# A two-layer encoder trunk: gains packed with the first x tiles on a second DMA queue, rotary tables on VectorE, the residual fetched during the second projection, and the last output block written by column chunks

## The chip, the cores and the metric

The kernel runs on one core of a Trainium2 chip. A core has a matmul engine (TensorE; PE in the profile, with its weight loads as PEld), VectorE (DVE), ScalarE (ACT), GpSimd (POOL), a queue that issues transfers (SyncE; SP), and 16 DMA engines that move data between HBM and the on-chip memory (SBUF). Matmuls write to PSUM, from where DVE or ACT read. The engines run side by side and wait for each other on semaphores. The metric is the time of one execution in microseconds (us); lower is better.

## The reference

The input is 256 tokens of width 2048 in float32. Two layers are computed; each adds a mixer and then a gated MLP to the residual x. In the first layer:

```python
h = rms_norm(x, norm_mix[layer])
proj = h @ w_in_ab[e]           # pooling channels | 12 query heads | 4 key heads | 4 value heads
q = apply_rope(rms_norm(q, q_norm[e]), cos, sin)
k = apply_rope(rms_norm(k, k_norm[e]), cos, sin)
pool_out = multiscale_pool(u, pool_w[e], pool_scale[e])
att_out = blocked_gqa(q, k, v)
x = x + concat(pool_out, att_out) @ w_out_ab[e]
x = x + conv_ffn(rms_norm(x, norm_ffn[layer]), w_up, conv_w, conv_b, w_down)
```

The second layer has an mLSTM mixer in the place of the attention and the same kind of MLP. All weights are read once, 410 MB in all.

## The kernel before

**Numbers.** The matmuls take a reduced float32 type (fp32r). To keep precision, each operand is written as a high part and a low part, and each product is three matmuls: high x high, high x low, low x high. So every weight that comes from HBM is first split: ACT casts it to the high part (L87), DVE subtracts that from the weight to get the low part (L88).

**Weights.** `Stream` reads the weights as chunks of 128 x 1024 floats (512 KB) in the order of use. `load` (L78) issues a chunk's transfer on SP's queue into one of 6 buffers `w`, `split` makes the two parts in one of 4 buffers `hl`, and `next` gives a chunk to the matmuls, after it has loaded up to 5 chunks and split 1 or 2 ahead. A moving chunk serves two slices of 128 input features: 12 matmuls of 512 columns, in kproj, qproj, vproj and the down projections.

**The start.** ACT's queue fetches the norm gains, `gcol` (32 KB, L176). SP's queue fetches the transposed x in eight transfers of 256 KB, two feature slices each (L178), with the first weight chunks between them; the first chunk comes in halves. Five matmuls on a zeroed tile (L215) run meanwhile. `Norm.parts` makes the high part (ACT, L251) and the low part (DVE, L252) of a slice of x times its gain. The scale of the norm, one factor per token, is applied after the projections. kproj (the keys) is the first projection, then qproj of the first four heads, vproj, and the other eight query heads.

**During kproj and after it.** When kproj's chunks have been issued, the program reads the residual, x with tokens on the partitions, in four transfers of 512 KB (L578), sums the squares of each block on ACT (`squares`, L259), and reads the first constants (L581) and the rotary tables `katt` (L583). POOL multiplies the tables by the q and k gains (L588). The `k_block` then squares the key heads on ACT (`hsq_k`, L391), rotates them on DVE (L400 to L403, `rot_k`), gets the norm's scale from the sums of squares (DVE, with one power on POOL, L198), scales (`rot_k`, L425), transposes on PE (`tr_k`, L434) and splits into `kt`. A `q_block` does the same for four query heads, and then `head` does scores, softmax, a transposition of the probabilities (`ptr`, L475) and the product with v.

**What sets the order.** The order on PE is written out by hand. `Weave` keeps small tasks (blocks, heads) as generators with a due time in estimated us; each time that a group of matmuls is written, `tick` advances the clock and may put one due step between. A `yield 5.5` is such an estimate. On the other engines a planner sets the order, except where the program pins it: ACT and DVE are pinned up to the end of kproj. A queue is served in order, so what stands behind a waiting instruction waits too. SP has at most eight transfers on their way, since each semaphore is waited for before it is used again.

**The end.** The down projection of the second MLP writes four blocks of 512 columns. The last, `down_end`, does all matmuls of the first 128 tokens, adds to x (DVE, L880) and writes out (L881), and then those of the other 128 tokens, with two additions and two writes of 256 columns. Both token halves lie in one PSUM tile, and in the program the matmuls of the second half wait for the addition of the first.

Of the kernel before, what the change touches and what calls it, by code (L numbers as in the profile page):

```python
# [9 lines left out]
F32 = mybir.dt.float32  # L10
# [6 lines left out]
P = 128  # L17
D = 2048
S = 256
KT = D // P  # L20
# [44 lines left out]
class Stream:  # L65
# [15 lines left out]

    def split(self):
        i = self.n_split
        w, n = self.w.pop(i)
        hl = self.spool.tile([P, 2, CH * P], F32R, tag="hl", name=f"hl{i}")
        for c in range(0, CH * P, n):
            self.nc.scalar.copy(hl[:, 0, c : c + n], w[:, c : c + n])  # L87
            self.nc.vector.tensor_sub(hl[:, 1, c : c + n], w[:, c : c + n], hl[:, 0, c : c + n].bitcast(F32))  # L88
        self.hl[i] = hl
        self.n_split += 1  # L90
# [62 lines left out]
@with_exitstack  # L153
def trunk(ctx: ExitStack, tc: tile.TileContext, xT, xn, gains, call, catt, cml, wgate, weights, out):
    nc = tc.nc
# [24 lines left out]
    ctx.enter_context(tc.manual_schedule(engines={mybir.EngineType.PE}))  # L180

    wv = Weave()
# [3 lines left out]
    def gain(n, k):  # L186
        c = n * KT + k
        return gcol[:, c : c + 1]
# [19 lines left out]

    warm = actp.tile([P, 512], F32, tag="B0", name="warm")
    v.memset(warm, 0.0)  # L210
# [3 lines left out]
    for i in range(WARM):  # L214
        pe.matmul(wps[:, :256], warm[:, :P], warm[:, :256], start=True, stop=True, skip_group_check=True)  # L215

    class Norm:
# [31 lines left out]
        def parts(self, j, src):  # L249
            n = self.n  # L250
            a.activation(self.xx[:, j, 0, :], src, AF.Copy, scale=gain(n, j))  # L251
            v.scalar_tensor_tensor(  # L252
                self.xx[:, j, 1, :], src, gain(n, j),
                self.xx[:, j, 0, :].bitcast(F32), ALU.mult, ALU.subtract)
# [62 lines left out]
    def mov_group(act, name, width=512, before=None, after=None):  # L317

        ps = mmp.tile([P, 2, width], F32, tag="mm", name=name)
        per = CH * P // width  # L320
        hl = None
        for k in range(KT):
            if k % per == 0:
                before and before(k)
                hl = st.next()
                after and after(k)
            src = act(k)
            c = (k % per) * width
            for t in range(2):
                xh, xl = src[:, 0, t * P : t * P + P], src[:, 1, t * P : t * P + P]  # L330
                o = ps[:, t, :]
                first, last = k == 0 and (width == 512 or t == 0), k == KT - 1 and (width == 512 or t == 1)
                mm(o, xh, hl[:, 0, c : c + width], first, False)
                mm(o, xh, hl[:, 1, c : c + width], False, False)
                mm(o, xl, hl[:, 0, c : c + width], False, last)
            wv.tick(1.29 * width / 512)
        return ps
# [33 lines left out]
    def attention_layer(norm, nxt):  # L371
        with ExitStack() as es:
# [11 lines left out]
            def block(ps, ti, dst, name):  # L384
# [32 lines left out]
                rq = None  # L417
                if name == "k":
                    fin = norm.finish()
                    yield next(fin)  # L420
                    rq = scales()
                    yield 4.0
                    for t in range(2):
                        r4 = rot[:, t, :].rearrange("p (h d) -> p h d", h=4)
                        v.tensor_mul(r4, r4, rq[:, 4 * t : 4 * t + 4].unsqueeze(2).to_broadcast([P, 4, P]))  # L425
                    yield 3.0
# [18 lines left out]
            def head(h, qt, hh, kt, vt, rq):  # L445
# [51 lines left out]
            def ahead(k):  # L497
                if k + 3 < KT:
                    norm.parts(k + 2, a_x[:, k + 2])
                    norm.parts(k + 3, a_x[:, k + 3])  # L500

            done = set()
# [77 lines left out]
            norm.blocks = NB  # L580
            nc.sync.dma_start(cst[:, :C_CONV], call[:, :C_CONV])  # L581
            kc = tp.tile([P, A_PW], F32, tag="rot", name="katt")
            nc.sync.dma_start(kc, catt[:, :A_PW])  # L583

            for i in range(4):
                gn = kc[:, A_QN + i * P : A_QN + (i + 1) * P]
                tr = kc[:, A_COS + (i % 2) * 2 * P : A_COS + (i % 2 + 1) * 2 * P]
# [10 lines left out]
            v.tensor_sub(vt[:, 1], vf, vt[:, 0].bitcast(F32))  # L598
            nc.sync.dma_start(cst[:, C_CONV:], call[:, C_CONV:])

# [231 lines left out]
    def ffn_layer(layer, norm, nxt):  # L832
        with ExitStack() as es:
# [31 lines left out]
            def down_end(gt, b, kts):  # L865

                ps = mmp.tile([P, 2, 512], F32, tag="mm", name="end")
                hls = [st.next() for _ in range(len(kts) // 2)]
                for t in range(2):
                    for k in kts:  # L870
                        c = k % 2 * 512
                        wh, wl = (hls[k // 2][:, j, c : c + 512] for j in range(2))
                        xh, xl = (gt[:, k, j, t * P : t * P + P] for j in range(2))
                        mm(ps[:, t], xh, wh, k == kts[0], False)
                        mm(ps[:, t], xh, wl, False, False)
                        mm(ps[:, t], xl, wh, False, k == kts[-1])
                    for c in range(0, 512, 512 // (1 + t)):
                        n = 512 // (1 + t)
                        xs = x[:, t, b * 512 + c : b * 512 + c + n]
                        v.tensor_add(xs, xs, ps[:, t, c : c + n])  # L880
                        nc.sync.dma_start(out[:, t, b * 512 + c : b * 512 + c + n], xs)  # L881

# [201 lines left out]
```

## Time and profile before

| what | value |
|---|---|
| time, median of 3 runs | 2217.97 us (2217.95 to 2218.12) |
| the profiled execution's time | 2218.25 us |
| its span in the profile | 2216.0 us |
| PE busy | 2205.2 us (100%) |
| PEld busy | 1887.1 us (85%) |
| DVE, ACT, POOL busy | 1527.6, 1169.5, 33.4 us |
| DMA | 415.45 MB, mean 187 GB/s |

The span goes from the first to the last event that the profiler saw on the core; the time also has what lies around it. A matmul's end is modelled, so a busy PE is not a PE at its peak. In a row of the timeline stand the start, the length, the engine, the line of the program, the operation with its output and inputs, the count, and in brackets how long the engine idled before it and who released it. The chain of work that ended last goes back from the last instruction to what released each step. The list of waits sums who waited for whom, as a total, a count and the longest.

### The profile page before, as it was taken

The numbers are of one execution on the slowest core, as the hardware profiler recorded it, in microseconds if no ns is written. First come the engines' busy times: TensorE is split into PE (matmuls) and PEld (weight loads), VectorE is DVE, ScalarE is ACT, GpSimd is POOL, SyncE is SP. The second block draws the span as 40 slices with busy tenths as digits, with TensorE's granted clock in tenths as the row PEclk, the third lists the DMA queues.
The fourth block names the chain that finished last, engine by engine and source line by source line (L and its number), as shares of the span: only waits on it lengthen the run. The fifth ranks groups of instructions, "written<-read, shape, count | busy, mean of one in ns | idle before, by whom it ended". The sixth has DMA issues, their size and how long they took to land.

```text
span 2216.0 us, 30515 instructions
## 1 busy us (share of the span) xinstructions
PE 2205.2 (100%) x11650; PEld 1887.1 (85%) x11650; DVE 1527.6 (69%) x2174; ACT 1169.5 (53%) x1662; POOL 33.4 (2%) x39
## 2 busy tenths in 40 slices
PE   8999999999999999999999999999999999999999
PEld 7888888888888888888888889888888888888887
DVE  7676677776676767666777676667777677676764
ACT  6665555554554545455554554455555455454542
POOL 1011000000000000000000000000000000000000
PEclk9999999999999999999999999999999999999999
DMA  8555566666666666654566555556656666666664
GB/s 317 167 165 163 177 190 189 191 190 192 190 191 190 191 191 189 196 188 156 178 193 186 180 183 171 184 178 190 190 190 190 190 190 191 190 190 190 190 191 141
DMA packets 117877, 415.45 MB, mean 187 GB/s; under 512 B 13115, under 2 KB 15587, under 8 KB 117731
## 3 DMA queue, kind: packets, MB, share of 16 engines
q1 hardware_dynamic: 114656, 410.02, 58.5%
q10 hardware_dynamic: 3074, 3.48, 0.7%
q8 instruction: 91, 1.49, 0.3%
q14 instruction: 56, 0.45, 0.1%
HBM read 411.31 MB, written 2.14 MB: 187 GB/s over the span
## 4 chain that ended last, share of the span: by engine, by line
PE 98%; ACT 1%; DVE 1%; DMA 0%; issue 0%; SPq 0%; DVEq 0%; ACTq 0%
PE up L191 44%; PE dn L191 21%; PE op L191 8%; PE mk L191 4%; PE mq L191 4%; PE mo L191 4%; PE mv L191 4%; PE qproj L191 3%; PE vproj L191 1%; PE kproj L191 1%; PE qk L191 1%; PE av L191 1%; PE end L191 1%; PE pool L191 0%; PE xt L242 0%; PE ov L191 0%
## 5 line engine op out<-in xcount | busy, mean ns | idle before, releaser
L88 DVE TENSOR_TENSOR hl<-w,hl 128x1024 fp32r<-128x1024 f32 (+1 forms) x769 | 937.7, 1220 | 470.7 <-ACT hl L87 469.1
L87 ACT CAST hl<-w 128x1024 fp32r<-128x1024 f32 (+1 forms) x769 | 806.7, 1050 | 683.7 <-PE dn L191 241.2
L191 PE MATMUL up<-xx,hl 128*128 128x512 f32 (+1 forms) x5632 | 984.2, 337 | 0.0
L191 PEld LDWEIGHTS up<-xx,hl 128*128 128x128 f32 x5632 | 857.9, 188 | 125.8
L191 PE MATMUL dn<-hl,g 128*128 128x512 f32 x2064 | 471.3, 389 | 0.0
L191 PEld LDWEIGHTS dn<-hl,g 128*128 128x128 f32 x2064 | 386.2, 188 | 79.5
L342 ACT COPY tb_up<-up 128x512 f32<-128x512 f32 x88 | 51.7, 587 | 154.0 <-PE up L191 154.0
L343 DVE TENSOR_TENSOR tb_up<-up,tb_up 128x512 f32<-128x512 f32 x88 | 60.9, 692 | 97.0 <-ACT tb_up L342 97.0
L854 ACT ACTIVATE y<-tb_up,cst 128x256 f32<-128x256 f32 x176 | 96.4, 595 | 46.9 <-DVE tb_up L850 46.9
L191 PE MATMUL mk<-xx,hl 128*128 128x512 f32 (+1 forms) x512 | 92.4, 338 | 0.0
L191 PE MATMUL mq<-xx,hl 128*128 128x512 f32 (+1 forms) x512 | 92.0, 337 | 0.0
L191 PE MATMUL op<-hl,cat 128*128 128x512 f32 x384 | 91.7, 393 | 0.0
L191 PE MATMUL mo<-hl,xx 128*128 128x512 f32 (+1 forms) x480 | 91.6, 348 | 0.0
L191 PE MATMUL mv<-hl,xx 128*128 128x512 f32 x384 | 89.6, 391 | 0.0
L191 PE MATMUL op<-hl,mcat 128*128 128x512 f32 x384 | 89.5, 392 | 0.0
L191 PEld LDWEIGHTS mq<-xx,hl 128*128 128x128 f32 x512 | 79.3, 188 | 11.7
L191 PEld LDWEIGHTS mk<-xx,hl 128*128 128x128 f32 x512 | 79.1, 188 | 11.4
L191 PEld LDWEIGHTS mo<-hl,xx 128*128 128x128 f32 x480 | 76.5, 190 | 10.6
L191 PEld LDWEIGHTS mv<-hl,xx 128*128 128x128 f32 x384 | 71.7, 188 | 14.8
L191 PEld LDWEIGHTS op<-hl,mcat 128*128 128x128 f32 x384 | 71.4, 188 | 14.6
L191 PEld LDWEIGHTS op<-hl,cat 128*128 128x128 f32 x384 | 70.9, 188 | 14.1
L857 DVE SCALAR_TENSOR_TENSOR y<-tb_up,cst,y 128x255 f32<-128x255 f32 x176 | 76.9, 479 | 0.0
(207 smaller groups left out, 1293.3 us busy)
## 6 DMA issues: line engine op xcount, KB each, us to landing
w<-in_up SPq DMA_DIRECT2D x352, 512.0 KB, 3.6
w<-in_dn SPq DMA_DIRECT2D x176, 512.0 KB, 4.0
w<-in_m_in SPq DMA_DIRECT2D x128, 512.0 KB, 3.6
w<-in_a_in SPq DMA_DIRECT2D x47, 512.0 KB, 4.1
w<-in_a_out SPq DMA_DIRECT2D x32, 512.0 KB, 3.4
w<-in_m_out SPq DMA_DIRECT2D x32, 512.0 KB, 3.4
xT<-in_xT SPq DMA_DIRECT2D x8, 256.0 KB, 6.9
x<-in_xn SPq DMA_DIRECT2D x4, 512.0 KB, 8.6
```

The costliest lines, as they stand in the source:

```text
L87: self.nc.scalar.copy(hl[:, 0, c : c + n], w[:, c : c + n])
L88: self.nc.vector.tensor_sub(hl[:, 1, c : c + n], w[:, c : c + n], hl[:, 0, c : c + n].bitcast(F32))
L191: pe.matmul(out_, lhsT, rhs, start=start, stop=stop, skip_group_check=True)
L342: a.copy(tb, ps[:, :, 1, :])
L343: v.tensor_add(tb, ps[:, :, 0, :], tb)
L854: a.activation(y[:, j, :], u[:, j, :], AF.Identity, scale=cw(tl, 1), bias=cw(tl, 3))
L857: v.scalar_tensor_tensor(y[:, j, 0 : S - 1], u[:, j, 1:S], cw(tl, 2), y[:, j, 0 : S - 1], ALU.mult, ALU.add)
```

## The change

- The gains and the first two slices of x are packed in one array `gx`, read with one transfer on ACT's queue into `gx0`; the next two slices of x follow on that queue. POOL copies the gains to `gcol`; the first two slices take their gains from `gx0`.
- SP's queue starts with the first two weight chunks, both in halves. The rest of x and the weights follow in turn.
- The very first cast, of half a chunk, is on DVE. The first six matmuls of kproj go by kind (both token halves high x high, then high x low, then low x high). The low part of the first slices is made between the two halves of the first chunk (`then`).
- The zeroed tile for the first matmuls is a quarter of x, 256 columns.
- `katt` and the first constants are read during kproj (`tables`, at k = 6), and DVE makes the table products when k = 14.
- The residual is read in four steps, two at k = 12 and 14 of kproj and two at k = 0 and 2 of qproj (`x_in`), and its squares are summed at k = 2 to 8 of qproj (`squares`). The k block waits for them (`norm.blocks == NB`) behind its rotation. SP, ACT and DVE are pinned up to the end of kproj, SP also in qproj.
- Heads 7 to 11 have a step of 6.5 in place of 5.5 ahead of their transposition.
- `down_end` does all but the last two slices for both token halves, then finishes in three pieces (128 tokens of 512 columns, 128 of 256, 128 of 256), each followed by its addition and its write.

```diff
-    def split(self):
+    def split(self, then=None):
...
         for c in range(0, CH * P, n):
-            self.nc.scalar.copy(hl[:, 0, c : c + n], w[:, c : c + n])
+            (self.nc.vector.tensor_copy if i + c == 0 else self.nc.scalar.copy)(hl[:, 0, c : c + n], w[:, c : c + n])
             self.nc.vector.tensor_sub(hl[:, 1, c : c + n], w[:, c : c + n], hl[:, 0, c : c + n].bitcast(F32))
+            then and then(c // n)
...
-    nc.scalar.dma_start(gcol, gains)
-    for i in range(8):
-        nc.sync.dma_start(a_x[:, 2 * i : 2 * i + 2, :], xT[:, 2 * i : 2 * i + 2, :])
-        st.n_load < 5 and st.load(2 if i == 0 else 1)
+    gx0 = actp.tile([P, NG + 2 * S], F32, tag="B0", name="gx0")
...
+    nc.scalar.dma_start(gx0, gx)
+    nc.scalar.dma_start(a_x[:, 2:4, :], xT[:, 0:2, :])
+    st.load(2)
+    st.load(2)
+    for i in range(2, 8):
+        nc.sync.dma_start(a_x[:, 2 * i : 2 * i + 2, :], xT[:, 2 * i - 2 : 2 * i, :])
+        st.n_load < 5 and st.load()
...
-    warm = actp.tile([P, 512], F32, tag="B0", name="warm")
+    warm = x[:, 0, 0:256]
...
+            terms = [(t, i, j) for t in range(2) for i, j in ((0, 0), (0, 1), (1, 0))]
+            if before and k == 0:
+                terms.sort(key=lambda e: e[1:])
...
                 if name == "k":
+                    yield from wv.wait(lambda: norm.blocks == NB)
                     fin = norm.finish()
...
-                yield 5.5
+                yield 5.5 if h < 7 else 6.5
...
+            def x_in(b):
+                nc.sync.dma_start(x[:, :, b * 512 : b * 512 + 512], xn[:, :, b * 512 : b * 512 + 512])
+
+            def squares(k):
+                if k < 4:
+                    x_in(k // 2 + 2)
+                if 2 <= k < 10:
+                    norm.squares(k // 2 - 1)
+                if k == 8:
+                    norm.blocks = NB
+                if k == 10:
+                    nc.sync.dma_start(cst[:, C_CONV:], call[:, C_CONV:])
+
+            def tables(k):
+                if k == 6:
+                    nc.sync.dma_start(kc, catt[:, :A_PW])
+                    nc.sync.dma_start(cst[:, :C_CONV], call[:, :C_CONV])
+                if k >= 12:
+                    x_in(k // 2 - 6)
+                if k == 14:
+                    for i in range(4):
...
+                        v.tensor_mul(tab[:, i], tr.rearrange("p (t d) -> p t d", t=2), bc(gn, 2))
...
-            with tc.manual_schedule(engines={mybir.EngineType.Activation, mybir.EngineType.DVE}):
-                norm.parts(0, a_x[:, 0])
-                st.ahead(0, 0)
-                norm.parts(1, a_x[:, 1])
-                st.sa = 1
-                ps = mov_group(xx, "kproj", 512, ahead)
-                st.sa = 2
+            g.tensor_copy(gcol, gx0[:, :NG])
+            srcs = [(j, gx0[:, NG + j * S : NG + j * S + S], gx0[:, j : j + 1]) for j in range(2)]
+            norm.high(*srcs[0])
+
+            def then(j):
+                norm.low(*srcs[j])
+                if j == 0:
+                    norm.high(*srcs[1])
+
+            st.split(then)
+            st.sa = 1
+            ps = mov_group(xx, "kproj", 512, ahead, tables)
+            st.sa = 2
+            first.close()
...
-            for b in range(NB):
-                nc.sync.dma_start(x[:, :, b * 512 : b * 512 + 512], xn[:, :, b * 512 : b * 512 + 512])
-                norm.squares(b)
...
-                g.tensor_mul(tab[:, i], tr.rearrange("p (t d) -> p t d", t=2), bc(gn, 2))
...
-            wv.add(q_block(mov_group(xx, "qproj0"), 0, 5.5))
+            with tc.manual_schedule(engines={mybir.EngineType.SP}):
+                ps = mov_group(xx, "qproj0", after=squares)
+            wv.add(q_block(ps, 0, 5.5))
...
-                for t in range(2):
-                    for k in kts:
...
+                for k in kts[:-2]:
+                    if k % 2 == 0:
+                        hl = st.next()
+                    for t in range(2):
+                        terms(t, k, hl, 0, 512)
+                hl = st.next()
+                for t, c0, c1 in ((0, 0, 512), (1, 0, 256), (1, 256, 512)):
+                    for k in kts[-2:]:
+                        terms(t, k, hl, c0, c1)
+                    xs = x[:, t, b * 512 + c0 : b * 512 + c1]
+                    v.tensor_add(xs, xs, ps[:, t, c0:c1])
+                    nc.sync.dma_start(out[:, t, b * 512 + c0 : b * 512 + c1], xs)
```

More of the change, by code (lines that the diff above doesn't have):

```diff
@@ L153, in trunk @@
 @with_exitstack
-def trunk(ctx: ExitStack, tc: tile.TileContext, xT, xn, gains, call, catt, cml, wgate, weights, out):
+def trunk(ctx: ExitStack, tc: tile.TileContext, gx, xT, xn, call, catt, cml, wgate, weights, out):
     nc = tc.nc
@@ L214, in trunk @@
     for i in range(WARM):
-        pe.matmul(wps[:, :256], warm[:, :P], warm[:, :256], start=True, stop=True, skip_group_check=True)
+        pe.matmul(wps[:, :256], warm[:, :P], warm, start=True, stop=True, skip_group_check=True)
     class Norm:
@@ L598, in attention_layer @@
             v.tensor_sub(vt[:, 1], vf, vt[:, 0].bitcast(F32))
-            nc.sync.dma_start(cst[:, C_CONV:], call[:, C_CONV:])
             def v_done():
@@ L867, in down_end, with terms @@
                 ps = mmp.tile([P, 2, 512], F32, tag="mm", name="end")
-                hls = [st.next() for _ in range(len(kts) // 2)]
-                for t in range(2):
-                    for k in kts:
[L871 to L881, printed above, removed]
+                n = len(kts)
+                def terms(t, k, hl, c0, c1):
+                    wh, wl = (hl[:, j, k % 2 * 512 + c0 : k % 2 * 512 + c1] for j in range(2))
+                    xh, xl = (gt[:, k, j, t * P : t * P + P] for j in range(2))
+                    mm(ps[:, t, c0:c1], xh, wh, k == kts[0], False)
+                    mm(ps[:, t, c0:c1], xh, wl, False, False)
+                    mm(ps[:, t, c0:c1], xl, wh, False, k == kts[-1])
+                for k in kts[:-2]:
[10 more added lines that the diff above has]
+                    nc.sync.dma_start(out[:, t, b * 512 + c0 : b * 512 + c1], xs)
             def down(c, gt, last):
@@ L1055 @@
     m_in, m_out = _ml_chunks(i["w_in_c"][0], i["w_out_c"][0])
+    xT = i["x"][0].T.reshape(KT, P, S).transpose(1, 0, 2)
     arrays = {
-        "xT": i["x"][0].T.reshape(KT, P, S).transpose(1, 0, 2), "gains": gains,
+        "gx": np.concatenate([gains, xT[:, 0:2].reshape(P, 2 * S)], axis=1), "xT": xT[:, 2:],
         "xn": i["x"][0].reshape(2, P, D).transpose(1, 0, 2),
@@ L1079 @@
     with tile.TileContext(nc, schedule_with_timeline_sim=True) as tc:
-        trunk(tc, t["xT"], t["xn"], t["gains"], t["call"], t["catt"], t["cml"], t["wgate"], weights, o)
+        trunk(tc, t["gx"], t["xT"], t["xn"], t["call"], t["catt"], t["cml"], t["wgate"], weights, o)
     r = _run(nc, [{f"in_{k}": val for k, val in arrays.items()}], core_ids=[0])
```

30 lines of the change are left out of this document (15 added, 15 removed).

## The prediction

> **What bounds the kernel now.** I read the page's engine totals first, then busy time by stage, then the chain of work that ended last, then who waited for whom. One engine is the kernel: the matmul engine is busy 2205.2 of 2216.0 us, so only its idle time, some 11 us, and its start and its tail can be won.
>
> ```profile
> PE 2205.2 (100%) x11650; PEld 1887.1 (85%) x11650; DVE 1527.6 (69%) x2174; ACT 1169.5 (53%) x1662; POOL 33.4 (2%) x39
> ```
>
> By stage (us from the span's start, then PE, PEld, DVE, ACT and POOL busy with counts, clock, DMA share, GB/s):
>
> ```profile
> 5.60:11.00 5.40, 4.02 (x15) 2.46 (x14) 3.77 (x7) 4.07 (x8) 0.00 (x0) 1.00 0.94 359
> 11.00:30.13 19.13, 19.13 (x84) 15.84 (x85) 13.20 (x21) 16.33 (x33) 0.58 (x1) 1.00 1.04 413
> 30.13:39.05 8.92, 6.22 (x26) 4.27 (x25) 8.24 (x17) 7.61 (x21) 2.90 (x5) 1.00 0.80 310
> 55.28:2200.25 2144.97, 2144.29 (x11402) 1839.27 (x11401) 1484.91 (x2100) 1132.49 (x1591) 24.66 (x25) 1.00 0.59 185
> ```
>
> Between 55.28 and 2200.25 the matmul engine idles 0.68 us in all. The change can therefore act in three places: before 11 us, between 30 and 39 us, and after 2200 us. The chain (start, length, what; the dn row is a stretch of pure matmuls) and the waits say what holds each:
>
> ```profile
> 8.64 1.05 ACT hl L87
> 9.72 1.24 DVE hl L88
> 11.00 19.14 PE kproj L191 x83
> 30.23 0.38 ACT hsq_k L391 x2
> 32.99 0.94 ACT hl L87
> 37.86 1.15 DVE hl L88
> 39.05 16.39 PE qproj L191 x71
> 1991.38 43.53 PE dn L191 x192
> ```
>
> ```profile
> PE ptr L475 <- ACT pr L466: 0.6, 1, 0.6
> PE end L191 <- DVE x L880: 0.8, 1, 0.8
> ```
>
> At 11.00 the matmul engine gets its second weight chunk: transfer, cast on ACT, subtraction on DVE, matmul. At 30.13 kproj ends and ACT squares kproj's heads (hsq_k) before it casts the next chunk, so qproj starves until 39.05. One matmul of 512 columns takes 43.53 / 192 = 0.2267 us, a chunk of 12 takes 2.72. From the matmul at 11.00 to the one at 39.05 lie 108 matmuls = 24.5 us of work in 28.05 us: 3.5 us are lost there.
>
> **The change, part by part.**
>
> *qproj's starving (the largest term).* In the new order ACT casts chunks 8, 9 and 10 ahead of the first hsq_k, and chunk 11 after two of the eight. The residual's 2 MB, which stood in SP's queue ahead of chunk 9, stand behind chunk 11 and then one block between two chunks. A chunk needs 512 KB in 2.72 us, with a residual block 1 MB, 377 GB/s, under the 413 of the second row above. Gain 3.5, all of it as long as nothing new is late. If half of one gap of 1.2 (cast and subtraction of one chunk, 30.13 to 39.05) stays, it is 2.9; that is my near end. What is late next is the k block itself, below.
>
> *The first chunks.* Rows, with the start, the length and in brackets the idle time before and its releaser:
>
> ```profile
> 4.41 0.51 ACT L251 ACTIVATE xx<-xT,gcol 128x256 fp32r<-128x256 f32 x1 [1.73 <-DMA gcol<-in_gains]
> 4.93 1.25 ACT L87 CAST hl<-w 128x512 fp32r<-128x512 f32 x2
> 5.58 1.32 DVE L88 TENSOR_TENSOR hl<-w,hl 128x512 fp32r<-128x512 f32 x2
> 8.64 1.05 ACT L87 CAST hl<-w 128x1024 fp32r<-128x1024 f32 x1 [1.25 <-DMA w<-in_a_in]
> 9.60 0.90 ACT L251 ACTIVATE xx<-xT,gcol 128x256 fp32r<-128x256 f32 x2
> 10.57 1.05 ACT L87 CAST hl<-w 128x1024 fp32r<-128x1024 f32 x1
> 11.65 1.22 DVE L88 TENSOR_TENSOR hl<-w,hl 128x1024 fp32r<-128x1024 f32 x1
> 14.45 1.05 ACT L87 CAST hl<-w 128x1024 fp32r<-128x1024 f32 x1 [0.17 <-DMA w<-in_a_in]
> ```
>
> Ahead of the first matmul stand 256 KB of x, 32 of gains and 256 of weights, 544 KB, both before and after; ahead of the end of chunk 1 stand 1568 KB both times. So the second queue by itself moves no byte forward; SP's queue loses two calls for x and gains one for chunk 1's halves; ACT issues one call more, in the 1.73 us that it idles before 4.41. What helps is that chunk 1 now comes in halves: its first 256 KB land 256 / 359 = 0.7 us before 8.62, near 7.9. Cast of a half 0.62, subtraction 0.69: its second matmul runs at about 9.3 instead of 11.00, 1.7 earlier. The second half (landed 8.62, cast to 9.25, subtracted by 9.95) is needed at 10.5 and is not late. Then chunk 2 binds: ACT does two activations after 9.25 (0.90), casts at 10.15 if the data is there (before, it was there at 10.57 without a wait), 1.05, subtraction 1.22: second matmul between 12.5 and 12.9, against 11.00 + 12 x 0.2267 = 13.72 before. Gain 0.8 to 1.2; chunk 3 (subtracted about 14.7, needed 15.2) and chunk 4 (its cast waited for data until 14.45, subtracted 16.7, needed 18) don't bind. I take 1.1. Ends: 0, if the two queues only make x and weights late together, and 1.7, if chunk 2 is on time. The move of the first cast to DVE and the sorted first six matmuls act before 9.3 and are hidden by it; the smaller warm tile too. The gains' copy on POOL (64 columns) sits between gx and the third activation, with over 1 us of room.
>
> The Trainium skill, page DMA: Bandwidth & Descriptors, section "Issuing engines are not separate DMA queues", says that issuing from several engines saves only the sequencer's issue time; by it alone the start would gain nothing but that. The byte count above agrees with it, and no row of before shows two large queues at once.
>
> *Tables on DVE, squares later, k block waits (a new cost).* The four table products leave POOL for DVE. Their nearest DVE row, an addition of 128x256, takes 0.42 (the chain's row at 2212.24 below): 1.7 in all, between chunk 8's and 9's subtraction. Chunks 8 to 10 are ahead there, so cost nothing; without that cover 1.7. But the k block now waits for the norm, and the norm for squares spread over qproj.
>
> ```profile
> 22.84 0.63 ACT L259 ACTIVATE sq<-x 128x512 f32<-128x512 f32 x1
> 23.59 0.63 ACT L259 ACTIVATE sq<-x 128x512 f32<-128x512 f32 x1
> 29.55 0.70 POOL L198 TENSOR_TENSOR ry_n<-rv_n,mhalf 128x2 f32<-128x2 f32 x1 [28.60 <-DVE rv_n L196]
> 41.32 3.49 DVE L88 TENSOR_TENSOR hl<-w,hl 128x1024 fp32r<-128x1024 f32 x3
> 41.50 4.82 POOL L198 TENSOR_TENSOR ry_qk<-rv_qk,mhalf 128x8 f32<-128x8 f32 x1 [8.46 <-DVE rv_qk L196]
> 48.37 1.29 DVE L425 TENSOR_TENSOR rot_k<-rot_k,re_qk 128x512 f32<-128x512 f32 x2
> 68.57 1.64 POOL L198 TENSOR_TENSOR ry_qq<-rv_qq,mhalf 128x8 f32<-128x8 f32 x1 [22.26 <-DVE rv_qq L196]
> ```
>
> Call T the end of kproj. ACT from T: eight hsq_k of about 0.4, eight squares of 0.75 and four casts of 1.05 = 13.4, in that queue without a hole. DVE then: sums and root with its power on POOL (0.70), to T+14.6; subtractions of chunks 15 and 16 and seven small operations, to T+18.8; there the power for the k heads goes to POOL, 1.64 behind one subtraction of 1.2, T+21.6; then small operations, one more subtraction and the two scalings of 1.29: T+25.05. The matmul engine wants rot_k after nine chunks, T+24.5. So a wait of 0.5 appears where there was none (tr_k). Behind it on PE stand vproj and everything else. Ends: 0, if the power gets ahead of the subtraction, and 2.4, if the power takes 4.82 as at 41.50, where three subtractions without a gap ran beside it. I take 0.5, because the new order has one subtraction there. The q block's rotation comes out at T+34.1 against a transpose at T+35.9: nothing.
>
> The Trainium skill, page SBUF — State Buffer, section "Who interferes with whom", says that a DVE instruction with two SBUF inputs and a GpSimd one that reads SBUF shut each other out, whoever comes first. By it the 4.82 is 1.64 plus waiting; this case's rows fit, the long one ending 1.5 after the subtractions. It speaks against pushing the k block close to its user; by it the sum would be the 0.5 or, three in a row, the 2.4.
>
> *Longer step for heads 7 to 11.* The one late transposition, 0.61 us (0.6 in the waits), belongs to such a head and gets about 0.4 us more matmuls ahead of it. Between 0 and 0.6; and a like loss, -0.6, since heads and q blocks fall differently. I take a gain of 0.3.
>
> *The last block.*
>
> ```profile
> 126.54 0.71 PE sc L191 x6
> 2205.72 0.69 DVE L880 TENSOR_TENSOR x<-x,end 128x512 f32<-128x512 f32 x1 [3.02 <-PE end L191]
> 2206.47 5.74 PE L191 MATMUL end<-hl,g 128*128 128x512 f32 x24 [0.78 <-DVE x L880]
> 2212.24 0.75 DVE L880 TENSOR_TENSOR x<-x,end 128x256 f32<-128x256 f32 x2 [5.83 <-PE end L191]
> ```
>
> ```profile
> 2212.24 0.42 DVE x L880
> ```
>
> Before, the second row half of the block waits for the addition of the first (0.78, and 0.3 more: 24 matmuls take 5.74 from rest against 5.44); at the end come two additions, 0.42 the first and 0.33 more for the second. In the new order matmuls into the one tile wait for DVE twice: after t = 0 (again 0.78 + 0.3) and between the column halves (0.42 + 0.06 + 0.3 = 0.78); six 256-column matmuls cost 0.71, so splitting is free. In return the 0.33 after the last matmul goes. Cost 0.78 - 0.33, about 0.4, less what SP's earlier issue may save: 0.35. Ends: -0.4, if the wait between the halves does not come, and +0.6.
>
> **Sum:** -1.1 - 3.5 + 0.5 - 0.3 + 0.35 = -4.05 us. The profiled execution took 2218.25, 2.25 outside its span and 0.28 above the median 2217.97. From the median: 2213.9. A change under 0.2%, 4.4 us, is what measurement hardly tells from none, so below 2213.5 counts as faster: the forecast lies just inside "same".
>
> **Rivals.** (a) Everything fits: 1.7 at the start, no wait at tr_k, the whole 0.6 at the heads: -1.7 - 3.5 - 0.6 + 0.35 = -5.45, 2212.5. For it: DVE and ACT have slack in every stage; against it: chunk 2's cast, which can hardly start at 9.7. (b) The second queue does not do what it says, x and weights hold each other up, the start gains nothing: 2215.0. The equal byte counts speak for it, the halved chunk against it. (c) The power stands behind a row of subtractions (4.82): 2.4 instead of 0.5, 2215.8. (d) Slower: the rotary table lands late, and the products at the head of DVE's queue hold back the subtractions of chunks 9 onward.
>
> ```profile
> 18.75 0.33 SPq L583 DMA_DIRECT2D katt<-in_catt  x1
> katt<-in_catt SPq DMA_DIRECT2D x1, 512.0 KB, 10.4
> ```
>
> Chunk 9's subtraction is needed at about 31.7; less 1.2 and 1.7, the table must be there at 28.8, and each us more costs one; it decides against the kernel past 37. Before, it landed at 29.15, behind the residual; now about 6.7 MB precede it, 2.1 of them in by 8.6, the rest at 413 GB/s: 20 to 22. So (d) needs 15 us of delay that nothing shows; as 2221 us.
>
> **Chances.** Forecast 0.43, (a) 0.25, (b) 0.14, (c) 0.11, (d) and its like 0.07. The forecast's own range, 2213.1 to 2214.7, reaches under 2213.5 for a third: faster 0.25 + 0.14 = 0.39, same 0.54, slower 0.07. The range takes in (a) to (c): 2212.0 to 2216.6, with the qproj term's near end of 2.9 and 2.4 at tr_k inside it.
>
> **What would show it.** Right: no idle matmul engine between kproj and vproj over 0.2 us; the second matmul of chunk 1 near 9.3 and of chunk 2 at 12.5 to 12.9; kproj's end near 29; a wait of PE's tr_k for DVE's rot_k of about 0.5; two waits of "end" for DVE, 0.8 and 0.5. Wrong: qproj still waiting for casts, katt's products preceded by a DMA wait, a chunk 1 that lands after 8.6, or new waits between 40 and 200 us where heads and q blocks were rearranged.

## The result, and the profile after

| | before | after |
|---|---|---|
| median of 9 runs | 2218.00 us (2217.89 to 2218.78) | 2212.03 us (2211.79 to 2212.42) |
| ratio after / before | | 0.9973, 95% interval 0.9963 to 0.9983 |
| profiled execution, its span | 2218.25, 2216.0 us | 2211.96, 2209.7 us |

The change makes the kernel 5.97 us faster, 0.27% (0.17% to 0.37% by the interval); all nine executions lie below all nine of before. By the prediction's own line of 2213.5 it counts as faster, to which it gave 0.39, and not as same, its likeliest call at 0.54. The median lies at the low end of the predicted range (2212.0 to 2216.6), 0.03 us inside it, while the runs spread over 0.63: that it falls inside is partly luck. The forecast of 2213.9 was 1.9 us too slow.

Engine totals of the changed kernel (the page's first part):

```profile
PE 2203.7 (100%) x11656; PEld 1886.9 (85%) x11656; DVE 1527.5 (69%) x2180; ACT 1169.1 (53%) x1662; POOL 27.7 (1%) x36
```

PE is still all of it; its idle time went from about 11 us to 6. Busy time by stage of the changed kernel (window in us, its length, PE, PEld, DVE, ACT, POOL busy with counts, clock, DMA share, GB/s):

```profile
11.00:28.27 17.27, 17.19 (x76) 13.93 (x75) 15.40 (x23) 11.71 (x17) 0.00 (x0) 1.00 1.03 415
28.27:50.03 21.76, 21.76 (x98) 18.02 (x97) 15.73 (x33) 16.19 (x40) 2.35 (x2) 1.00 0.92 334
50.03:2193.58 2143.55, 2143.55 (x11402) 1838.89 (x11401) 1486.22 (x2102) 1132.82 (x1591) 24.59 (x25) 1.00 0.59 185
2193.58:2209.70 16.12, 11.47 (x55) 9.08 (x53) 3.95 (x6) 1.06 (x1) 0.00 (x0) 0.99 0.17 65
```

From 28.27 to 2193.58 PE has no idle time at all. Before, it idled 2.70 us between kproj and vproj, where its matmuls also took 0.84 longer (22.60 against 21.76), and 0.68 behind vproj's start. The row of before for kproj's end to vproj's start:

```profile
30.14:55.44 25.30, 22.60 (x97) 17.85 (x97) 20.77 (x34) 12.93 (x26) 7.71 (x6) 1.00 0.80 264
```

The chain of the changed kernel (start, length, what), the parts at which stages begin and end:

```profile
3.07 6.42 DMA w<-in_a_in
...
11.88 16.39 PE kproj L200 x71
28.27 21.76 PE qproj L200 x96
50.03 2.73 PE vproj L200 x12
...
267.19 32.97 PE up L200 x189
```

The same mark of before, the first long stretch of the MLP's up projection, in its chain:

```profile
273.86 26.24 PE up L191 x150
```

With the prediction's rows of before (kproj's end 30.14, vproj's start 39.05 + 16.39 = 55.44, the last block 2200.25, the span's end 2216.0) the whole difference is placed:

| stage | before | after | difference | predicted |
|---|---|---|---|---|
| start to kproj's end | 30.14 | 28.27 | -1.87 | -1.1 |
| kproj's end to vproj's start | 25.30 | 21.76 | -3.54 | -3.5, and +0.5 for tr_k |
| vproj's start to the mark of up | 218.42 | 217.16 | -1.26 | -0.3 |
| that mark to the last block | 1926.39 | 1926.39 | 0.00 | 0 |
| last block to the end | 15.75 | 16.12 | +0.37 | +0.35 |
| sum | 2216.0 | 2209.7 | -6.30 | -4.05 |

The one wait of PE that is left in the changed kernel behind its first matmuls on zeroes (total, count, longest):

```profile
PE end L200 <- DVE x L925: 1.3, 2, 0.8
```

The transposition's wait (ptr, 0.6) is gone, and the one wait of the last block has become two. The start of the changed kernel in its timeline: the first matmul's weight load, the casts of chunk 1's halves, the second matmul of chunk 1, the cast of chunk 2:

```profile
5.25 0.30 PEld L200 LDWEIGHTS kproj<-hl,xx 128*128 128x128 f32 x2 [0.44 <-ACT xx L263]
...
6.92 1.34 ACT L87 CAST hl<-w 128x512 fp32r<-128x512 f32 x2
...
8.77 2.61 PEld L200 LDWEIGHTS kproj<-hl,xx 128*128 128x128 f32 x12 [0.41 <-DVE hl L88]
...
9.52 1.05 ACT L87 CAST hl<-w 128x1024 fp32r<-128x1024 f32 x1 [0.34 <-DMA w<-in_a_in]
```

### The profile page after: what moved, and what is told of

It reads as the page before. It is cut to its first block, busy times and chain, and to the rows that moved or that the text cites. A ratio compares the mean times of both kernels' runs of the same rounds, so it can differ in the third digit from the quotient of the medians.

```text
span 2209.7 us, 30530 instructions
## 1 busy us (share of the span) xinstructions
PE 2203.7 (100%) x11656; PEld 1886.9 (85%) x11656; DVE 1527.5 (69%) x2180; ACT 1169.1 (53%) x1662; POOL 27.7 (1%) x36
## 3 DMA queue, kind: packets, MB, share of 16 engines
q10 hardware_dynamic: 3218, 4.01, 0.7%
## 4 chain that ended last, share of the span: by engine, by line
PE 99%; DMA 0%; DVE 0%; SPq 0%; ACT 0%; issue 0%
PE up L200 44%; PE dn L200 21%; PE op L200 8%; PE mk L200 4%; PE mq L200 4%; PE mo L200 4%; PE mv L200 4%; PE qproj L200 3%; PE pool L200 1%; PE vproj L200 1%; PE kproj L200 1%; PE end L200 1%; PE qk L200 1%; PE av L200 1%; PE xt L251 0%; PE ov L200 0%
```

## The experiments

The median of before was 2218.00 beside the changed kernel and 2218.11 to 2218.32 beside the experiments, so medians that differ by 0.3 or less say little; where so little is at stake, the stage in the profile decides. The part of the time that lies outside the span also differs, from 1.87 to 2.55 us between executions of the changed kernel and of the experiments. So the median span of all executions is given where it says something else than the time. "After" is the changed kernel, median time 2212.03, median span 2209.8 (2209.7 to 2209.9).

### The start: one queue

```diff
-    nc.scalar.dma_start(gx0, gx)
-    nc.scalar.dma_start(a_x[:, 2:4, :], xT[:, 0:2, :])
+    nc.sync.dma_start(gx0, gx)
     st.load(2)
+    nc.sync.dma_start(a_x[:, 2:4, :], xT[:, 0:2, :])
     st.load(2)
```

> The changed kernel with x's first part and its second part issued on SP's queue like the weights (order: x with gains, two halves of chunk 0, second part of x, two halves of chunk 1, third part of x, chunk 2). The same bytes in the same order, one queue. In the changed kernel the second matmul of chunk 2 ran at 11.88 and kproj ended at 28.27. Theory A (the second queue fills the dip in the DMA rate between 5 and 8 us): the dip comes back, chunk 2's cast goes from 9.5 to about 10.5, kproj ends 0.8 to 1.9 later (29.1 to 30.1), the whole 2212.8 to 2213.9. Theory B (the dip was the small rows of the gains by themselves, which now ride with x): kproj ends at 28.3 to 28.5, the whole within 0.3 of 2212.0. Theory C (only chunk 1's halves matter): like B. The prediction's own rule, that the second queue moves no byte forward, is also like B.

Measured: 2213.06 (2212.77 to 2213.84), 1.03 above after. Its chain, and its row for 2 to 8 us:

```profile
4.01 6.36 DMA w<-in_a_in
...
12.77 16.43 PE kproj L200 x71
```

```profile
2.00:8.00 6.00, 6.00 (x18) 4.51 (x16) 2.33 (x5) 2.46 (x7) 0.24 (x1) 1.00 0.96 315
```

The same row of before, and then of after:

```profile
2.00:8.00 6.00, 6.00 (x18) 4.39 (x17) 2.90 (x6) 3.62 (x8) 0.00 (x0) 1.00 0.88 296
```

```profile
2.00:8.00 6.00, 5.96 (x21) 4.12 (x20) 3.28 (x7) 4.34 (x9) 0.31 (x1) 1.00 0.98 348
```

kproj ends at 29.20 instead of 28.27: theory A's size, 0.93 us (0.8 by the median spans, 2210.6 against 2209.8). Chunk 2's transfer is issued 0.94 later (4.01 against 3.07), which is two calls of 0.47 on SP's queue, and takes as long to land (6.36 and 6.42). From 2 to 8 us the rate is 315 GB/s instead of 348; before it was 296. Issue time and rate move together here, and this run doesn't part them.

### The start: one call more on ACT's queue

```diff
     for i in range(2, 8):
-        nc.sync.dma_start(a_x[:, 2 * i : 2 * i + 2, :], xT[:, 2 * i - 2 : 2 * i, :])
+        (nc.scalar if i == 2 else nc.sync).dma_start(a_x[:, 2 * i : 2 * i + 2, :], xT[:, 2 * i - 2 : 2 * i, :])
```

> The changed kernel with one more of x's parts, the third, issued on ACT's queue instead of SP's; the same bytes. On one queue chunk 2's transfer was issued at 4.01 and landed 6.36 later, on two at 3.07 and 6.42 later. Theory I (SP's issue, 0.47 a call, is what the second queue saves): chunk 2's transfer is issued at about 2.6, its cast starts 0.3 to 0.5 earlier than 9.52 and kproj ends at 27.8 to 28.0; 2211.5 to 2211.8. Theory R (the bytes' rate, 400 GB/s once both queues run, is what lands chunk 2): the cast stays at 9.4 to 9.6 or comes later, as x's third part now passes ahead of chunk 1; kproj's end 28.2 to 28.8, 2212.0 to 2212.6.

Measured: 2212.12 (2211.83 to 2212.50), after's time. Its chain, and the cast of chunk 1's second half in its timeline:

```profile
2.11 6.46 DMA w<-in_a_in
...
12.28 16.41 PE kproj L200 x71
```

```profile
8.59 0.62 ACT L87 CAST hl<-w 128x512 fp32r<-128x512 f32 x1 [0.18 <-DMA w<-in_a_in]
```

SP does issue chunk 2 one call earlier, near 2.6 instead of 3.07, but nothing is won; the median span is after's 2209.8. The profiled execution is the run's slowest. The transfer that binds in it is chunk 1's second half, issued at 2.11 and landed 6.46 later, at 8.57; in after it took 5.5 and was cast by 8.26. Chunk 2 takes 7.2 and lands near 9.8, where after has 9.49. In the run with both edits at the end, whose start is the same, the two take 6.0 and 6.8, and kproj ends at 28.38. That fits theory R: with 256 KB of x ahead on the other queue, these transfers land later by at least what the call saved.

### The start: gains by themselves, and chunk 1 whole

```diff
-    nc.scalar.dma_start(gx0, gx)
+    nc.scalar.dma_start(gx0[:, :NG], gx[:, :NG])
+    nc.scalar.dma_start(gx0[:, NG:], gx[:, NG:])
```

> The changed kernel with the gains and x's first part, one transfer of 128 rows, read by two on ACT's queue: the gains with 256 B a row, then x. Theory B (small rows of their own cost the DMA engines time): packets under 512 B in the first 12 us go from 176 towards 296 and the first matmul (5.25) and chunk 2's cast (9.5) come 0.3 to 1 later, kproj's end 28.6 to 29.3, the whole 2212.3 to 2213.0. Theory A (second queue) and theory C (halves): no more than 0.2 later, 2212.0 to 2212.2.

Measured: 2212.55 (2211.85 to 2213.74), 0.5 above after, as theory B has it, but with a spread of 1.9 where after's is 0.6. The profiled execution (2213.66) is of the late end. Its chain:

```profile
1.65 7.29 DMA xT<-in_xT
...
11.23 19.17 PE kproj L201 x83
```

Here it is x's second part that lands late, at 8.94, and kproj ends at 30.40. Three of the ten executions are that long (spans 2211.7 and 2211.8); the median span is 2210.6, 0.8 above after's. So packing the gains with x is worth 0.5 to 0.8 us in the median, and up to two in the executions in which x is late. Theory B's reason isn't shown by this: the edit also adds a call, which puts x's second part at 1.65 instead of 1.18 on ACT's queue. With three transfers of ACT and five of SP on their way, eight in all, chunk 2's issue waits for the gains to land, until 3.78 instead of 3.07. Small rows and the extra call aren't parted.

```diff
-    st.load(2)
+    st.load()
```

> The changed kernel with weight chunk 1 in one piece again: one transfer, one cast of 1.05, one subtraction of 1.24 in place of two halves each. Theory C (the halves bring the gain): the second matmul of chunk 1 goes from 8.77 to about 9.5 to 9.9 (its last byte near 7.5, cast, subtraction), kproj's end 0.7 to 1.1 later, 2212.7 to 2213.1. Theory A or B (the data's earlier arrival brings it, and chunk 2 binds anyway): chunk 1 a little later but chunk 2 as late as before, at 11.9 with the wait ahead of chunk 1's matmul in place of a part of the later one; kproj's end within 0.4 of 28.27, the whole 2212.0 to 2212.4.

Measured: 2212.29 (2212.07 to 2212.66), 0.26 above after by the time, 0.55 by the median span (2210.35). Its chain, and the same transfer, chunk 1's, in the chain of before:

```profile
1.64 5.96 DMA w<-in_a_in
...
9.99 19.11 PE kproj L200 x83
```

```profile
2.58 6.04 DMA w<-in_a_in
```

Chunk 1 binds again, as it did before the change: its second matmul runs at 9.99 instead of 8.77, and kproj ends at 29.10, 0.83 later than after's 28.27. In the stage that is theory C (0.7 to 1.1); the time moved by less. Its first matmul is 0.49 later than after's (5.74 against 5.25), but that isn't on the chain, and it does not move kproj's end: in the run of the next section, with after's start, the first matmul is at 5.56 and kproj ends at 28.28.

Against before, chunk 1 is issued at 1.64 instead of 2.58 (two calls of 0.47) and lands at 7.60 instead of 8.62, and kproj ends 1.04 earlier, without any halves. So the start's 1.87 divide into 1.04 without the halves and 0.83 with them.

### The heads' step

```diff
-                yield 5.5 if h < 7 else 6.5
+                yield 5.5
```

> The changed kernel with the step of heads 7 to 11 put back from 6.5 to 5.5, all else as changed. The stretch from vproj's start to the layer's first up matmul was 1.26 us shorter in the changed kernel, the 0.6 us wait for one late transposition among it. Theory H (the longer step does it): the wait of ptr for pr comes back, 0.6 in the list of waits, and the stretch is 0.6 to 1.3 longer, 2212.6 to 2213.3. Theory S (the earlier q and k blocks and the different order before do it, the step is idle): no such wait, the same stretch within 0.2, 2212.0 to 2212.2. The prediction gave the step 0 to 0.6 with a like loss possible.

Measured: 2211.71 (2211.61 to 2211.81). Its chain:

```profile
5.56 22.72 PE kproj L200 x96
28.28 21.76 PE qproj L200 x96
50.04 2.73 PE vproj L200 x12
...
267.23 32.97 PE up L200 x189
```

The stretch from vproj to the mark is 217.19, after's is 217.16, and its span is after's 2209.7 (median span 2209.8 as well; the 0.32 by which its time is lower lies outside the span): theory S. No wait of ptr returns. The step is idle, and the 1.26 us of that stage come from elsewhere.

### The residual: squares and loads early, loads alone early

```diff
+            for b in range(NB):
+                x_in(b)
+                norm.squares(b)
+            norm.blocks = NB
             wv.add(k_block(ps))
...
-                if k < 4:
-                    x_in(k // 2 + 2)
-                if 2 <= k < 10:
-                    norm.squares(k // 2 - 1)
-                if k == 8:
-                    norm.blocks = NB
...
-                if k >= 12:
-                    x_in(k // 2 - 6)
```

> The changed kernel with the residual's four loads and its sixteen squares issued right after kproj, as in the kernel before; the order of the other work as changed. Theory Q (the residual and its squares ahead of the chunks starve qproj): the stretch from kproj's end to vproj's start, 21.76 in the changed kernel and 25.30 before, goes back by most of the 3.54; 2214.5 to 2215.6. Theory K (it was the k heads' squares ahead of two casts, and the residual's bytes are hidden): the stretch grows by less than 1; 2212.0 to 2213. Sub-question for the layer's pool stage: if the wait of one transposition there (0.6 before) returns, the residual's place in ACT's order is behind it.

Measured: 2214.91 (2213.96 to 2215.71), 2.9 above after. Its window from kproj's end to vproj, its ACT timeline, its waits of PE, its chain at the mark of up:

```profile
28.30:51.54 23.24, 22.41 (x98) 18.01 (x97) 19.71 (x39) 13.94 (x30) 2.34 (x2) 1.00 0.89 319
```

```profile
28.30 0.63 ACT L273 ACTIVATE sq<-x 128x512 f32<-128x512 f32 x1 [1.89 <-DMA x<-in_xn]
```

```profile
PE qproj L200 <- DVE hl L88: 0.8, 1, 0.8
PE ptr L490 <- ACT pr L481: 0.6, 1, 0.6
```

```profile
270.03 30.19 PE up L200 x173
```

Neither theory fits as it was put. qproj's stretch grows by 1.48 (23.24 against 21.76), between K's 1 and Q's 3.54: a square on ACT waits 1.89 for the residual's last block, and the next chunk's cast stands behind it. The matmul engine's wait is 0.83 of the 1.48; the other 0.65 is that the same matmuls take longer (22.41 against 21.76). The rest comes from where only the sub-question looked: the wait of ptr is back, and vproj to the mark is 270.03 - 51.54 = 218.49, before's 218.42 again. So the residual's place, not the heads' step, is what costs 1.3 us in the pool stage. This run sets `norm.blocks` ahead of the k block, so the k block's wait for the squares is void in it too; the two aren't parted.

```diff
-                if k < 4:
-                    x_in(k // 2 + 2)
...
-                if k >= 12:
-                    x_in(k // 2 - 6)
+                if k == 8:
+                    for b in range(NB):
+                        x_in(b)
```

> The changed kernel with the residual's four loads issued together after the ninth k step of kproj, ahead of chunk 10 on SP's queue; squares stay spread, though the planner then puts the eight k squares and four of the residual's between the casts of chunks 9 and 10. Against the run with everything early this parts bytes from ACT's order. If the bytes starve qproj (2 MB at 413 GB/s are 4.8 us ahead of chunk 10, with two to three chunks of 2.72 in store): a wait for w in ACT's casts and 1 to 3 us more, 2213 to 2215. If the bytes are hidden and ACT's order decides: 8 x 0.4 + 4 x 0.75 = 6.2 us between two casts with two chunks in store of 2.72 each: 0.8 to 2 more, the casts not waiting for data.

Measured: 2216.17 (2214.63 to 2216.59), 4.1 above after. Its chain, its ACT timeline around kproj's end, and its busy time in two windows:

```profile
5.82 22.49 PE kproj L200 x96
...
36.76 17.79 PE qproj L200 x71
54.55 2.73 PE vproj L200 x12
```

```profile
28.33 0.28 ACT L405 ACTIVATE hsq_k<-kproj 128x128 f32<-128x128 f32 x1 [4.16 <-PE kproj L200]
...
34.42 1.03 ACT L87 CAST hl<-w 128x1024 fp32r<-128x1024 f32 x1
```

```profile
36.00:38.00 2.00, 1.24 (x4) 1.05 (x4) 1.67 (x2) 2.00 (x5) 0.00 (x0) 0.59 0.08 29
38.00:40.00 2.00, 2.00 (x6) 1.58 (x6) 1.49 (x2) 2.00 (x4) 0.00 (x0) 0.55 0.87 279
```

The edit moves loads only; the changed order on ACT is the planner's answer to it. ACT idles 4.16 us until kproj ends, because the next instruction in its queue is the first hsq_k; then eight of those and four squares take from 28.33 to 34.42 before chunk 10 is cast. Neither this cast nor a later one of qproj waits for data. Chunk 10, issued at 20.24, lands 10.1 later, at 30.3; cast and subtraction (1.05 and 1.23) at once would have been done at 32.6, and the matmuls of chunks 8 and 9 last until 28.31 + 24 x 0.2267 = 33.75. So ACT's order starves qproj, and in these two runs the residual's bytes do so only where an instruction ahead of a cast waits for them. The size was wrong: from kproj's end at 28.31 to vproj at 54.55 are 26.24, 4.48 more than after's 21.76, instead of 0.8 to 2. Of that, 1.7 is the clock, granted at 0.59 and 0.55 between 36 and 40 us: 71 matmuls took 17.79 instead of 71 x 0.2267 = 16.10. The ten executions say the same: six with a mean clock of 0.999 have spans of 2214.2 to 2214.7, four with 1.000 have 2212.7 to 2212.9, 3.0 above after's. No ptr wait here: the early squares bring it, the early loads don't.

### The tables on POOL

```diff
-                        v.tensor_mul(tab[:, i], tr.rearrange("p (t d) -> p t d", t=2), bc(gn, 2))
+                        g.tensor_mul(tab[:, i], tr.rearrange("p (t d) -> p t d", t=2), bc(gn, 2))
```

> The changed kernel with the four products of the rotary tables on POOL, as before the change, at the same place. Theory N (as the prediction costed it: 4 x 0.42 on DVE behind chunks that are ahead, nothing on the path): within 0.2 of 2212.0, no wait of PE between kproj and vproj. Rival: the products run on POOL at several us each and the k block's power, behind them on POOL, comes later: a wait of tr_k for rot_k of 0.5 to 3, 2212.5 to 2215.

Measured: 2211.83 (2211.79 to 2211.92), span 2209.7 like after's. The products in this run and then in after (minimum, median and maximum in ns, then first and last start):

```profile
L542 POOL TENSOR_TENSOR tab<-katt x4: 732/1718/2877, 21.6 to 26.8; 128x256 f32<-128x256 f32 x4
```

```profile
L542 DVE TENSOR_TENSOR tab<-katt x4: 417/420/420, 23.8 to 24.8; 128x256 f32<-128x256 f32 x4
```

On POOL they take 6.9 us in all instead of 1.4, end at 28.6, long before the k block's power, and nobody waits. Theory N: this part of the change is worth nothing here.

### The last block

```diff
-                for k in kts[:-2]:
-                    if k % 2 == 0:
-                        hl = st.next()
-                    for t in range(2):
-                        terms(t, k, hl, 0, 512)
...
+                hls = [st.next() for _ in range(len(kts) // 2)]
+                for t in range(2):
+                    for k in kts:
...
```

> The changed kernel with the last block's loop of before: first row half whole, then the second, its addition in two column halves at the end. The prediction gave the new order +0.35 (before 15.75 from the last block's matmuls to the span's end, the changed kernel 16.12). By it this run is 0.35 to 0.4 faster than the changed kernel, 2211.6 to 2211.7, the tail 15.7 to 15.8. Rival: the tail's difference is that of two executions (the outputs' landing), and the run is within 0.1 of 2212.0.

Measured: 2211.84 (2211.63 to 2211.91). Its chain:

```profile
2193.61 5.45 PE end L200 x24
...
2199.83 5.75 PE end L200 x24
```

From 2193.61 to its span's end, 2209.4, are 15.79 us, against 16.12 in after and 15.75 before. The new order costs 0.33 here, as predicted; the median spans differ by 0.4 (2209.4 against 2209.8), the median times by 0.19, which by themselves would not show it.

```diff
-                ps = mmp.tile([P, 2, 512], F32, tag="mm", name="end")
+                pieces = ((0, 0, 512), (1, 0, 256), (1, 256, 512))
+                pss = [psp.tile([P, c1 - c0], F32, tag="ps", name=f"end{i}") for i, (t, c0, c1) in enumerate(pieces)]
...
-                    for t in range(2):
-                        terms(t, k, hl, 0, 512)
+                    for ps, (t, c0, c1) in zip(pss, pieces):
+                        terms(ps, t, k, hl, c0, c1)
```

> The changed kernel with the last block's three pieces in three PSUM tiles of their own, so that no matmul waits for DVE's read of another piece; the 256-column pieces run through all chunks. Theory W (the two waits of 0.78 and 0.51 and the slow restart of 0.3 behind each are the tail's price): no wait of end for DVE, the tail 14.2 to 14.7 in place of 16.12, 2210.1 to 2210.6. Rival: the split pieces' matmuls cost more than whole ones (48 pairs of 256 columns in place of 24 of 512, 0.01 to 0.03 each) or the end is set by the last addition and the output's landing alone: 0.3 to 0.9 gained, 2211.1 to 2211.7.

Measured: 2210.64 (2210.55 to 2210.76), ratio to before 0.9966 (0.9953 to 0.9979), 1.39 under after. Its chain:

```profile
2193.66 11.26 PE end L200 x72
...
2204.94 0.42 DVE x L925
```

No wait of end is left; the tail is 2208.2 - 2193.66 = 14.54 instead of 16.12, 1.58 less, and the median span (2208.2) is 1.6 under after's. Theory W. The price of the smaller pieces is 11.26 - 48 x 0.2267 = 0.4, inside the gain.

Both edits that might help together, the three tiles and x's third part on ACT's queue:

> Both together: three PSUM tiles in the last block and x's third part on ACT's queue. The two edits lie 2190 us apart, so their differences from the changed kernel should add: -1.39 of the tiles (2210.64 against 2212.03) and what the third part brings (-0.4 by theory I, 0 to +0.6 by theory R): 2210.2 or 2210.6 to 2211.2.

Measured: 2210.59 (2209.97 to 2210.69), the three tiles' time. The third part adds nothing here either; the version with the three tiles alone is the one to keep, 7.7 us under the median of before beside it (2218.32).

## Why the prediction was right or wrong

**qproj's starving: -3.5 predicted, -3.54 measured.** The work between the two marks was counted right, and all of the idle time went, 2.70 us, with the 0.84 by which the matmuls were slower. Of its two reasons, the casts ahead of hsq_k carry the weight: with ACT's order bad and no cast of qproj waiting for data, 4.48 us return, 1.7 of them through the clock. No cast of qproj waits for data in before either. The residual's 2 MB mattered where squares waited for them in ACT's queue; that the chunks' own bytes came late is shown in no run. (The prediction's 377 GB/s is 385: 1,048,576 bytes in 2.72 us, still under 413.)

**The wait of tr_k: +0.5 predicted, none measured.** From the changed kernel's timeline, POOL and then DVE:

```profile
45.70 1.64 POOL L207 TENSOR_TENSOR ry_qk<-rv_qk,mhalf 128x8 f32<-128x8 f32 x1 [3.78 <-DVE rv_qk L205]
```

```profile
45.72 1.27 DVE L88 TENSOR_TENSOR hl<-w,hl 128x1024 fp32r<-128x1024 f32 x1
...
49.97 1.29 DVE L440 TENSOR_TENSOR rot_k<-rot_k,re_qk 128x512 f32<-128x512 f32 x2
```

rot_k is done at 51.26, T + 23.0 where T + 25.05 was worked out, and PE wants it at 52.76: 1.5 us to spare. The power begins 1.4 earlier than worked out, and it runs beside the subtraction instead of behind it. That was the step's named lower end (0, the power gets ahead of the subtraction). The Trainium skill, page SBUF — State Buffer, section "Who interferes with whom", which the prediction set beside the 0.5, would have one of the two wait for the other. Here they start 0.02 apart and take 1.64 and 1.27, where the subtraction alone takes 1.22. POOL's spans are rough, so the rule isn't refuted, but this place doesn't show it.

**The start: -1.1 predicted, -1.87 measured.** The step that failed is "the second queue by itself moves no byte forward". The bytes ahead of each chunk are indeed the same, but they are asked for sooner: chunk 1 is issued two calls earlier, and in one piece, as before, it lands 1.02 earlier and ends kproj 1.04 earlier. That part holds the packing too. The halves of chunk 1, to which the whole gain was ascribed, bring the other 0.83. The prediction counted that SP loses two calls and gains one, and put no price on it; taking two calls back in the changed kernel, where chunk 2 binds, costs 0.93. The Trainium skill, page DMA: Bandwidth & Descriptors, section "Issuing engines are not separate DMA queues", says that issuing from several engines saves the sequencer's issue time and nothing else. The 0.94 by which chunk 2's issue moves agrees with it; the rate, which rose as well (348 GB/s instead of 296 from 2 to 8 us), is no part of the rule, and no run here parts the two. The mistake was to read "saves only the issue time" as zero, where the first transfers are issued one behind the other and every chunk's landing counts from its issue. Put back one at a time, the two calls cost 0.93, the halves 0.83 and the gains' packing 0.5 to 0.8, more than 1.87 in all, so these parts overlap. Chunk 2 binds, as predicted; its cast begins at 9.52, where 10.15 was expected, and its second matmul, expected at 12.5 to 12.9, runs at 11.88. kproj's end, expected near 29, is 28.27.

**Heads: -0.3 predicted, -1.26 measured.** Size and cause were both off. The longer step does nothing (217.19 against 217.16). The late transposition goes because the residual's squares moved, and comes back with them. And the stage loses more than the wait's row. Rows of before: the transposes behind the wait, and the whole stage; then the same of the changed kernel:

```profile
149.86 0.94 PE L475 MATMUL ptr<-cst,pr 128*128 128x128 f32 x4 [0.61 <-ACT pr L466]
```

```profile
55.44:273.86 218.42, 217.74 (x1122) 184.47 (x1121) 147.50 (x242) 132.06 (x261) 14.17 (x14) 1.00 0.53 168
```

```profile
145.41 0.60 PE L490 MATMUL ptr<-cst,pr 128*128 128x128 f32 x4
```

```profile
50.03:267.19 217.16, 217.16 (x1122) 184.28 (x1121) 149.13 (x244) 132.46 (x261) 14.08 (x14) 1.00 0.53 169
```

The 1122 matmuls of before lose 0.68 us of idle time and 0.58 of longer busy time (0.34 of it in these transposes). Their order differs between the two kernels, so the 0.58 need not all come from the wait; in qproj's stretch of the run with everything early, the order is the same, and a wait of 0.83 cost 1.48. The prediction charged the list's 0.6, though it had this second part right in the last block (0.78, and 0.3 more).

How the squares' place in the first 40 us moves a transposition 100 us later is shown only as far as this: it comes with another order of small tasks, and PE's order in that stage is another one. Which of the later steps carries it was not tried.

**The last block: +0.35 predicted, +0.37 measured** (0.33 with the old loop put back). The two waits came at 0.78 and 0.51. The new order was meant for less work after the last matmul, and one PSUM tile for all pieces gave back more than that.

**Together.** The term for the start was too small by 0.8, that for the heads by 1.0, and the 0.5 for tr_k was not there: 2.25 of the 6.30. All three errors lie on one side, and rival (a), "everything fits", at 2212.5, described the outcome best; the doubt held against it, that chunk 2's cast can hardly start at 9.7, was wrong (9.52).

## What to carry to other kernels

At a kernel's start, price each transfer's issue on its queue: the two calls that were moved off the busy queue were worth 0.9 us, and a third nothing: the chunks behind it took longer to land by as much. An in-order engine that feeds the bound one must not have an instruction that waits for something late ahead of the feed; that, not a transfer that came late, was the 3.5 us here. And a bound engine's wait costs more than its row in the list, so give work that should overlap its own PSUM tile: three tiles won 1.4 us (1.6 in the stage), where reordering within one tile lost 0.35.

## What was not expected of the hardware

- The clock falls after a short rest: with the loads alone early, PE idled 1.77 and 0.76 us with one matmul between, and the granted clock was 0.59 and 0.55 in the next two windows of 2 us, which cost 1.7 us. Before the change, three waits of about 1.1, 0.8 and 0.8 us between 32 and 39 us, with a dozen matmuls ahead of the last, left the clock at 1.00.
- The weight transfer that bound the start took 5.96 to 6.46 us from issue to landing in five kernels (5.96, 6.04, 6.36, 6.42, 6.46), on one queue or two, at 256 KB or 512 KB.
